# Cosine-similarity attention: five PSUM banks of scores, exponentials of 1536 and 1024 columns in turn, norm words moved into the second output bank, and the norms of 26 pairs summed on VectorE

## The chip, the core and the metric

The kernel runs on one core of one Trainium2 chip. The metric is the device time of one execution in microseconds (us). A core has five engines with instruction streams of their own: TensorE (PE in the profile, its weight loads PEld), VectorE (DVE), ScalarE (ACT), GpSimd (POOL) and SyncE (SP), which here only issues transfers. They meet through semaphores. TensorE writes its results to PSUM, which has 8 banks of 512 float columns on 128 partitions; the other engines read them there.

## The reference

For 8 batches of 12 heads, with 512 rows of 64 numbers each, the rows of Q and K are normalised, their products are divided by tau = 0.1 and go through a softmax, and V is averaged with the weights:

```python
batch, heads, seq, dim = 8, 12, 512, 64
Q_norm = Q / (np.linalg.norm(Q, axis=-1, keepdims=True) + 1e-10)
K_norm = K / (np.linalg.norm(K, axis=-1, keepdims=True) + 1e-10)
scores = np.einsum('bhqd,bhkd->bhqk', Q_norm, K_norm) / tau
weights = np.exp(scores - np.max(scores, axis=-1, keepdims=True))
weights = weights / (np.sum(weights, axis=-1, keepdims=True) + 1e-10)
out = np.einsum('bhqk,bhkd->bhqd', weights, V)
```

The scores are cosines times 10, so the kernel leaves out the maximum: no exponential can overflow.

## The kernel before

Two heads make a pair, and 48 pairs (0 to 47) follow each other as in a pipeline. The names below are those of the order in the code: a number after the name is the pair, then the part.

- LD and LV load Q, K and V of a pair (SyncE; the first K and pair 1 elsewhere). The buffers of Q and K hold 18 pairs.
- SQ squares Q and K (GpSimd, 1024 columns a pair).
- The sums of the squares over 64 columns come in two ways. For most pairs TensorE adds 16 slices with an identity matrix (SSQ, line 246) and VectorE adds the four columns that are left (RED, line 253). For the eight pairs in `DIRECT` VectorE reduces the squares itself in two instructions of 512 columns (line 240), and there is no SSQ.
- NEW, steps 0 to 5, is a reciprocal square root on VectorE, by a first guess from the bits and two rounds of refinement, for a group of one or two pairs (`GROUPS`). Steps 6 and later write the factors of Q and of K. The words lie in PSUM (`nps`, a bank of its own, five groups in turn) and SBUF (`ys`, `rk`).
- SCL multiplies Q (VectorE) and K (GpSimd) by their factors. TR transposes both on TensorE into the bank `xps`, and EVA copies them to SBUF on VectorE as `qt`. Seven pairs (`XT`) have K transposed by a transfer instead.
- SCO are the scores: for each head of the pair and each of four chunks c of 128 keys a matmul of 64 rows by 512 columns, one PSUM bank. The two heads lie on rows 0 to 63 and 64 to 127, so both can be in the array at once.
- EXP are the exponentials on ScalarE. SCO.s.c fills two banks (both heads of chunk c), EXP.s.c turns the 1024 columns into bf16 weights in `et`. There are two such couples of banks, so SCO.s.c waits for the exponential two before. `et` holds three pairs. Pair 0 has exponentials of 512 columns, and the last couple of pair 47 goes in three parts (`ENDS`, line 472).
- VC makes V bf16 and adds a column of ones (GpSimd). PV.s.h.t multiplies the weights with it: four matmuls of 65 columns for head h and 128 rows t, into the output banks `ops`, one per head. The 65th column is the sum of the weights.
- RCP takes its reciprocal, NRM multiplies (both VectorE), ST stores. PV of the next pair waits for NRM, since there is one set of output banks.

The eight banks are thus: four for scores, two for outputs, one for transposes and norm sums, one for norm words.

Nothing is scheduled at run time. `ORDER` spells out the operations of each engine in their order, and `schedule` and `run` (lines 46 and 60) turn the needs of each operation into waits. An operation that waits holds up all that stands behind it on its engine. At the start TensorE runs dummy matmuls (`warm`, `fill`, line 218).

Of the kernel before, what the change touches and what calls it, by code (L numbers as in the profile page):

```python
# [10 lines left out]
class Op:  # L11
# [6 lines left out]
    def __init__(self, key, eng, needs, emit, slot=None, take=None, until=None, hard=()):  # L18
# [3 lines left out]
        self.slot, self.take, self.until = slot, take, until  # L22
        self.sem, self.val, self.inc, self.used = None, 0, 0, False
# [6 lines left out]
class Program:  # L30
# [15 lines left out]
    def schedule(self):  # L46
# [3 lines left out]
        for e, ops in order.items():  # L50
            before = {}
# [74 lines left out]
def bass_cosine_similarity_attention_kernel(  # L126
# [28 lines left out]
    et = [sb(f"et{i}", [128, NT, 2, SEQ], bf16) for i in range(R_ET)]  # L155
# [11 lines left out]
    sc_ps = nc.alloc_psum_tensor("scps", [128, 4, SEQ], f32)  # L167
# [3 lines left out]
    n_ps = nc.alloc_psum_tensor("nps", [128, R_X, 6 * W], f32)  # L171
# [17 lines left out]

    def src(x, s):  # L190
        b, h = divmod(2 * s, NHEAD)
        return x[b, h : h + 2].rearrange("h (p t) d -> p h (t d)", t=NT)
# [7 lines left out]

    def scores_read(s, c):

        if s < 0:
            return None
        return ("EXP", s, c, 1) if s == 0 else ("EXP", s, c, 2) if (s, c) == (NP - 1, NT - 1) else ("EXP", s, c)

# [14 lines left out]
    for k in range(WARM):  # L221
        dummy(("warm", k), sc_ps[:, 3], ["wz", ("warm", k - 1) if k else None])
# [11 lines left out]
    def sums(s, dst, free):  # L234

        sqs = [k for k in (("SQ", s, 0), ("SQ", s, 1)) if k in P.ops]
        if s in DIRECT:
            for w in range(2):
                P.add(("RED", s, w), "dve", [sqs[min(w, len(sqs) - 1)], free],
                      lambda e, w=w: e.tensor_reduce(  # L240
                          out=dst(w), in_=sq[s % R_SQ][:, 8 * w : 8 * w + 8, :], axis=AX.X, op=ALU.add))
# [10 lines left out]
        P.add(("RED", s, 0), "dve", [("SSQ", s), free],  # L252
# [13 lines left out]
    def scaled(s, w, eng, r, needs):  # L266
# [5 lines left out]
                  in0=qk[iq][:, w].rearrange("p h (t d) -> p h t d", t=NT), in1=r, op=ALU.mult))  # L272
# [17 lines left out]
    def head():  # L290

        k_ps = o_ps[:, 0, :].bitcast(bf16).rearrange("p (t x) -> p t x", x=128)
        rq = [o_ps[:, 1, 384:388], sc_ps[:, 1, 0:4]]
        for h in range(2):
            for w, x, eng in ((0, Q, "sp"), (1, K, "act")):
                P.add(("LD", 0, w, h), eng, [], lambda e, w=w, x=x, h=h: e.dma_start(
                    out=qk[0][:, w, h], in_=src(x, 0)[:, h]), slot=f"first{w}{h}")
        for h in range(2):
# [15 lines left out]
            P.add(("SCL", 0, 0, h), "dve", [("EX", 0, 0, h)], lambda e, h=h, q_out=q_out, view=view: e.tensor_tensor(  # L314
# [32 lines left out]
    def norms(g):  # L347
# [20 lines left out]
        for k, step in enumerate(steps):  # L368
# [8 lines left out]
            P.add(("NEW", g, k), "dve", needs, step)  # L377
        for k, (i, j) in enumerate(k_runs(g), 7):
            P.add(("NEW", g, k), "dve",
                  [("NEW", g, 5)] + ([("SCL", p, 1) for p in range(first[g - R_X], first[g - R_X] + sizes[g - R_X])] if g >= R_X else []),  # L380
                  up(k_norms(g, i, j), m + 8 * i, m + 8 * j))

    def pair(s):
        g = group[s]
        iq, iv, iqt, iet, io = (s % r for r in (R_QK, R_V, R_QT, R_ET, R_O))
# [20 lines left out]
        if s == 1:  # L406
            rq = o_ps[:, 1, 384:392]
# [4 lines left out]
            r = xr[1][:, :] if eng == "pool" else o_ps[:, 1, 392:400]  # L412
# [13 lines left out]
        if s:  # L426
            nb = NT if s in XT else 2 * NT
            if s in XT:
                P.add(("XT", s), "sp", [("SCL", s, 1), *[key("SCO", s - R_QT, NT - 1, *y) for y in ((), (0,), (1,))]],
# [4 lines left out]
            P.add(("EVA", s), "dve", [("TR", s), *[key("SCO", s - R_QT, NT - 1, *y) for y in ((), (0,), (1,))]],  # L434
# [4 lines left out]
        last_pair = s == NP - 1  # L439
        for c in range(NT if s == 0 else 0):  # L440
            b = c % 2
            for h in range(2):
                P.add(("SCO", 0, c, h), "pe",
                      [("EVA", 0, 0, h), ("EVA", 0, 1, h), ("EXP", 0, c - 2, h) if c > 1 else None,
                       ("fill", FILL[0] - 1) if c == 1 and h and FILL[0] else None],
                      lambda e, b=b, c=c, h=h: e.matmul(  # L446
                          out=sc_ps[:, 2 * b + h, :], lhsT=qt[0][64 * h : 64 * h + 64, 1, c, :],
                          rhs=qt[0][64 * h : 64 * h + 64, 0, :, :], start=True, stop=True))
        for i, (c, h) in enumerate(START if s == 0 else ()):
# [3 lines left out]
                      out=et[0][:, c, h, :], in_=sc_ps[:, 2 * b + h, :], func=ACT.Exp,  # L453
                      scale=xr[0][:, NT * h + c : NT * h + c + 1]), hard=[("EX", 0, 1, h)])
        for c in range(NT if s else 0):
            b = c % 2

            def sco(e, c=c, b=b):
                for h in range(2):
                    last = e.matmul(  # L460
                        out=sc_ps[:, 2 * b + h, :], lhsT=qt[iqt][64 * h : 64 * h + 64, 1, c, :],
                        rhs=qt[iqt][64 * h : 64 * h + 64, 0, :, :], start=True, stop=True)
                return last

            P.add(("SCO", s, c), "pe",
                  [("SCO", s, c - 1) if c else None, ("EVA", s), key("XT", s),
                   scores_read(s, c - 2) if c >= 2 else scores_read(s - 1, c + 2)], sco)
            before = [("SCO", s, c), scores_read(s, c - 1) if c else scores_read(s - 1, NT - 1), key("PV", s - R_ET, 1, NT - 1)]
            if last_pair and c == NT - 1:
                for i, (h, lo, hi) in enumerate(ENDS):  # L470
                    P.add(("EXP", s, c, i), "act", before + [key("EXP", s, c, i - 1)],
                          lambda e, c=c, b=b, h=h, q=slice(128 * lo, 128 * hi): e.activation(
# [87 lines left out]
WARM = 17  # L560
# [177 lines left out]
```

## Time and profile before

| what | value |
|---|---|
| median of 3 runs | 192.63 us (192.46 to 193.04) |
| the profiled execution | 192.5 us |
| its span, first to last instruction | 190.8 us |
| granted TensorE clock, mean | 0.996 |
| bytes read and written | 37.75 MB, 12.58 MB |
| VectorE instructions, ScalarE instructions | 456, 214 |

The profile's groups read: line, engine, operation, output and input tiles, shape, count; then busy time in us and the mean ns of one; then the idle time of the engine just before them and what ended it. Timeline rows read: start in us, length in us, then the group and its count. Rows of windows give the stretch, its length, the busy time of each engine asked for with the number of instructions, the granted clock, the share of the transfer engines and GB/s. A row of waits reads: who waited, for whom, us in total, how often, the longest.

### The profile page before, as it was taken

The numbers are of one execution on the slowest core, as the hardware profiler recorded it, in microseconds if no ns is written. First come the engines' busy times: TensorE is split into PE (matmuls) and PEld (weight loads), VectorE is DVE, ScalarE is ACT, GpSimd is POOL, SyncE is SP. The second block draws the span as 40 slices with busy tenths as digits, with TensorE's granted clock in tenths as the row PEclk, the third lists the DMA queues.
The fourth block names the chain that finished last, engine by engine and source line by source line (L and its number), as shares of the span: only waits on it lengthen the run. The fifth ranks groups of instructions, "written<-read, shape, count | busy, mean of one in ns | idle before, by whom it ended". The sixth has DMA issues, their size and how long they took to land.

```text
span 190.8 us, 7108 instructions
## 1 busy us (share of the span) xinstructions
PE 178.1 (93%) x2943; PEld 116.5 (61%) x2943; DVE 149.1 (78%) x456; ACT 182.1 (95%) x214; POOL 163.3 (86%) x151
## 2 busy tenths in 40 slices
PE   7899999999998999999989899999999999999982
PEld 5466666656664666666646566566656666656551
DVE  1699987789788899679967988789789598976623
ACT  5699999999999999999999999999999999999991
POOL 6799989999999998999899999999899999970000
PEclk9999999999999999999999999999999999999998
DMA  5999999689999999999989999489375899210167
GB/s 170 300 359 351 351 355 368 177 277 322 375 361 282 311 339 366 239 349 347 365 274 283 353 356 379 134 247 342 105 248 170 248 363 352 66 55 3 55 212 233
DMA packets 55872, 51.71 MB, mean 271 GB/s; under 512 B 6944, under 2 KB 55712, under 8 KB 55840
## 3 DMA queue, kind: packets, MB, share of 16 engines
q1 hardware_dynamic: 55392, 50.48, 82.6%
q0 software_dynamic: 160, 0.52, 0.8%
q8 instruction: 23, 0.38, 0.8%
q10 hardware_dynamic: 288, 0.26, 0.4%
q14 instruction: 9, 0.07, 0.1%
HBM read 37.75 MB, written 12.58 MB: 264 GB/s over the span
## 4 chain that ended last, share of the span: by engine, by line
ACT 72%; PE 15%; POOL 5%; DVE 3%; DMA 2%; issue 1%; POOLq 0%
ACT et L476 72%; PE scps L460 4%; PE ops L492 3%; POOL sq L231 3%; PE xps L246 3%; DMA qk<-in_Q_dram 2%; PE xps L277 2%; POOL qn L270 1%; PE ops L218 1%; DVE qt L435 1%; POOL vb L481 1%; PE scps L446 1%; DVE ob L536 1%; DVE ob L506 0%; DVE nps L355 0%
## 5 line engine op out<-in xcount | busy, mean ns | idle before, releaser
L476 ACT ACTIVATE et<-scps 128x1024 bf16<-128x1024 f32 x187 | 172.0, 1149 | 0.6 <-PE scps L460 0.6
L231 POOL TENSOR_TENSOR sq<-qk 128x1024 bf16<-128x1024 f32 (+1 forms) x49 | 88.8, 1823 | 2.5 <-DMA qk<-in_Q_dram 2.2
L460 PE MATMUL scps<-qt 64*128 64x512 bf16 x376 | 73.3, 386 | 6.4 <-ACT et L476 4.5
L492 PEld LDWEIGHTS ops<-vb,et 128*128 128x128 bf16 x1504 | 53.3, 98 | 25.2 <-issue 18.7
L492 PE MATMUL ops<-vb,et 128*128 128x65 bf16 x1504 | 67.9, 194 | 0.2
L270 POOL TENSOR_TENSOR qn<-qk,rk 128x512 bf16<-128x512 f32 x44 | 45.4, 1043 | 3.2 <-DVE rk L359 2.9
L435 DVE COPY qt<-xps 128x1024 bf16<-128x1024 bf16 (+1 forms) x47 | 30.5, 648 | 6.3 <-PE xps L277 5.7
L506 DVE TENSOR_TENSOR ob<-ops,rd 128x512 f32<-128x512 f32 x47 | 32.4, 690 | 1.1
L460 PEld LDWEIGHTS scps<-qt 64*128 64x128 bf16 x376 | 18.5, 93 | 23.2 <-ACT et L476 9.2
L270 DVE TENSOR_TENSOR qn<-qk,nps 128x512 bf16<-128x512 f32 x48 | 32.1, 680 | 0.2
L481 POOL TENSOR_SCALAR vb<-vf 128x512 bf16<-128x512 f32 x48 | 29.6, 626 | 0.0
L277 PE MATMUL xps<-ident,qn 128*128 128x128 bf16 x348 | 27.5, 220 | 0.0
L246 PE MATMUL xps<-sq,ident 128*128 128x64 bf16 x624 | 25.0, 192 | 0.9 <-POOL sq L231 0.9
L246 PEld LDWEIGHTS xps<-sq,ident 128*128 128x128 bf16 x624 | 20.6, 97 | 8.2 <-issue 4.1
L277 PEld LDWEIGHTS xps<-ident,qn 128*128 128x128 bf16 x348 | 19.7, 98 | 8.3 <-issue 3.6
L504 DVE RECIPROCAL rd<-ops 128x8 f32<-128x8 f32 x47 | 9.7, 206 | 15.0 <-PE ops L492 14.1
L253 DVE TENSOR_REDUCE nps<-xps 128x16 f32<-128x64 f32 x38 | 8.7, 229 | 7.1 <-PE xps L246 6.8
L240 DVE TENSOR_REDUCE nps<-sq 128x8 f32<-128x512 bf16 x16 | 10.7, 680 | 0.0
L355 DVE SCALAR_TENSOR_TENSOR nps<-nps,ys 128x32 f32<-128x32 f32 (+1 forms) x48 | 9.3, 194 | 1.2
L354 DVE TENSOR_TENSOR nps<-nps,ys 128x32 f32<-128x32 f32 (+1 forms) x48 | 9.3, 193 | 0.9
L218 PE MATMUL scps<-warm_in 128*128 128x256 bf16 x23 | 5.1, 382 | 1.1 <-DVE warm_in L216 1.1
L452 ACT ACTIVATE et<-scps,xr 128x512 bf16<-128x512 f32 x8 | 4.8, 688 | 0.1
(54 smaller groups left out, 49.2 us busy)
## 6 DMA issues: line engine op xcount, KB each, us to landing
vf<-in_V_dram SPq DMA_DIRECT2D x48, 256.0 KB, 5.7
out_dram<-ob SPq DMA_DIRECT2D x47, 256.0 KB, 4.8
qk<-in_K_dram SPq DMA_DIRECT2D x46, 256.0 KB, 5.8
qk<-in_Q_dram SPq DMA_DIRECT2D x46, 256.0 KB, 6.0
qk<-in_Q_dram SPq DMA_DIRECT2D x2, 128.0 KB, 2.7
qk<-in_K_dram ACTq DMA_DIRECT2D x2, 128.0 KB, 2.9
qk<-in_Q_dram POOLq DMA_DIRECT2D x1, 256.0 KB, 4.7
qk<-in_K_dram POOLq DMA_DIRECT2D x1, 256.0 KB, 4.3
```

The source lines that it names most:

```text
L231: emit = lambda e: e.tensor_tensor(out=b, in0=a, in1=a, op=ALU.mult)
L240: lambda e, w=w: e.tensor_reduce(out=dst(w), in_=sq[s % R_SQ][:, 8 * w : 8 * w + 8, :], axis=AX.X, op=ALU.add))
L246: last = e.matmul(out=x_ps[:, 0:64], lhsT=ident[:, :], rhs=sq[s % R_SQ][:, :, 4 * k : 4 * k + 4], start=(k == 0), stop=(k == 15))
L270: lambda e: e.tensor_tensor(out=qn[iqn][:, w].rearrange("p t h d -> p h t d"), in0=qk[iq][:, w].rearrange("p h (t d) -> p h t d", t=NT), i ...
L277: last = e.transpose(dst[:, i, :], qn[s % R_QN][:, b // NT, b % NT].rearrange("p h d -> p (h d)"), ident[:, :])
L435: lambda e: e.tensor_copy(out=qt[iqt][:, :].rearrange("p w t x -> p (w t) x")[:, 0:nb], in_=tb[:, 0:nb]))
L460: last = e.matmul(out=sc_ps[:, 2 * b + h, :], lhsT=qt[iqt][64 * h : 64 * h + 64, 1, c, :], rhs=qt[iqt][64 * h : 64 * h + 64, 0, :, :], sta ...
L476: lambda e, c=c, b=b: e.activation(out=et[iet][:, c, :, :], in_=sc_ps[:, 2 * b : 2 * b + 2, :], func=ACT.Exp, scale=inv_tau))
L481: lambda e: e.tensor_scalar(out=vb[:, iq, :, :, 0:DIM].rearrange("p c h d -> p h c d"), in0=vf[iv][:, :, :].rearrange("p h (c d) -> p h c ...
L492: last = e.matmul(out=o_ps[:, h, 65 * t : 65 * t + 65], lhsT=et[iet][:, c, h, 128 * t : 128 * t + 128], rhs=vb[:, iq, c, h, :], start=(c = ...
L504: lambda e: e.reciprocal(out=rd[io][:, :], in_=grid[:, :, :, DIM]))
L506: lambda e: e.tensor_tensor(out=ob[io][:, :], in0=grid[:, :, :, 0:DIM], in1=rd[io][:, :].unsqueeze(3).to_broadcast([128, 2, NT, DIM]), op= ...
```

## The change

The needs of the work stay; the bank plan, the size of the exponentials, the place of the norm words, the way of some norm sums and all five orders are new.

1. *Scores.* Five banks instead of four. The 376 blocks (pair, chunk, head) of pairs 1 to 47, less the last two, are cut into 151 units of three and two blocks in turn, across the borders of chunks and pairs: `stream`. Even units have banks 0 to 2 and odd units 3 and 4. Units 0, 2, 4 and 150 (`TWO`) have two blocks. SCO.k and EXP.k are now those of unit k; the last two blocks are the unit Z, whose exponential goes in the same three parts as before. There are 72 exponentials of 1536 columns and 79 of 1024, with the 187 of 1024 gone.
2. *Weights.* `et` becomes six slots of five blocks. PV finds its block by `place`.
3. *Outputs and norm words.* The eight output tiles lie 65 columns wide in pairs every 149 columns, so that only the last (head 1, t = 3) is in the second output bank, at its first 65 columns. The norm words (four groups in turn) lie behind it in that bank. Since TensorE and VectorE would then use one bank, VectorE operations on the words are marked `shares`, and the last PV step of a pair waits for the last such operation ahead of the pair's RCP (`after`).
4. *Norm sums.* `DIRECT` has 26 pairs instead of 8, so 18 SSQ are gone and 36 reductions of 512 columns come for 18 of 64.
5. *Start.* 12 filler matmuls instead of 18, into a bank that pair 0 leaves free. On ScalarE and VectorE some of the first operations change places; `one` goes ahead of the loads on GpSimd's queue, and the loads of pair 1 and its squares go K first.

```diff
+                if o.shares:
+                    sharer = o.key
+                if o.after is not None and sharer is not None:
+                    self.ops[o.after].needs.append(sharer)
...
-    R_QK, R_V, R_SQ, R_QN, R_QT, R_ET, R_O = 18, 6, 6, 5, 5, 3, 8
+    R_QK, R_V, R_SQ, R_QN, R_QT, R_ET, R_O = 18, 6, 6, 5, 5, 6, 8
-    R_X = 512 // (6 * W)
+    R_X = 4
...
-    et = [sb(f"et{i}", [128, NT, 2, SEQ], bf16) for i in range(R_ET)]
+    et = sb("et", [128, R_ET, 5 * SEQ], bf16)
...
-    sc_ps = nc.alloc_psum_tensor("scps", [128, 4, SEQ], f32)
+    sc_ps = nc.alloc_psum_tensor("scps", [128, 5, SEQ], f32)
...
-    n_ps = nc.alloc_psum_tensor("nps", [128, R_X, 6 * W], f32)
+    n_ps = o_ps[:, 1, 65 : 65 + R_X * 6 * W].rearrange("p (g x) -> p g x", g=R_X)
...
+    def o_tile(h, t):
+        return o_all[:, 149 * t + 65 * h : 149 * t + 65 * h + 65]
...
+    blocks = [(s, c, h) for s in range(1, NP) for c in range(NT) for h in range(2)]
+    blocks, ends = blocks[:-2], blocks[-2:]
+    stream, place = [], {}
+    while sum(map(len, stream)) < len(blocks):
+        at, k = sum(map(len, stream)), len(stream)
+        stream.append(blocks[at : at + (2 if k % 2 or k in TWO else 3)])
...
+    def scores(k):
+        unit, part = stream[k], k % 2
+        bank = sc_ps[:, 3 * part : 3 * part + len(unit), :]
+        def sco(e):
+            for j, (s, c, h) in enumerate(unit):
+                rows = slice(64 * h, 64 * h + 64)
+                last = e.matmul(out=bank[:, j, :], lhsT=qt[s % R_QT][rows, 1, c, :], rhs=qt[s % R_QT][rows, 0, :, :],
+                                start=True, stop=True)
+            return last
...
+        P.add(("EXP", k), "act",
+              [("SCO", k), ("EXP", k - 1) if k else ("EXP", 0, *START[-1]), ("PV", gone, 1, NT - 1) if gone is not None else None],
+              lambda e: e.activation(
+                  out=et[:, (k // 2) % R_ET, lo : lo + SEQ * len(unit)], in_=bank, func=ACT.Exp, scale=inv_tau), width=len(unit))
...
-DIRECT = {36, 41, 11, 46, 16, 21, 26, 31}
+DIRECT = {36,41,11,46,16,21,26,31,8,13,19,24,29,34,38,44,10,18,23,28,33,40,43,14,20,25}
...
-FILL = (6, 12)
+FILL = 12
+TWO = {0,2,4,150}
```

The new order of TensorE around the units that the prediction speaks of:

```
SCO.5 SSQ.5 SCO.6 TR.3 PV.0.0.3 PV.0.1.0 PV.0.1.1 PV.0.1.2 PV.0.1.3 SSQ.6 SCO.7 SCO.8 SSQ.7 PV.1.0.0
```

A stretch of VectorE's new order, with copy, reciprocal and the steps of a square root in between:

```
EVA.21 RCP.17 NEW.11.7 NRM.17 RED.25.1 RED.25.0 SCL.22.0 NEW.12.0 RCP.18 NEW.12.1 NRM.18 SCL.23.0
```

More of the change, by code (lines that the diff above doesn't have):

```diff
@@ L11, with __init__ @@
 class Op:
-    def __init__(self, key, eng, needs, emit, slot=None, take=None, until=None, hard=()):
+    def __init__(self, key, eng, needs, emit, slot=None, take=None, until=None, hard=(), shares=False, after=None, width=0):
         self.key, self.eng, self.emit = key, eng, emit
@@ L251, in sums @@
         P.add(("SSQ", s), "pe", sqs + ["eye", ("warm", WARM - 1) if s == 1 else None], ssq, take="x", until=("RED", s, 0))
-        P.add(("RED", s, 0), "dve", [("SSQ", s), free],
+        P.add(("RED", s, 0), "dve", [("SSQ", s), *free], shares=s > 1, emit=
               lambda e: e.tensor_reduce(
@@ L452, in pair @@
                   lambda e, c=c, b=b, h=h: e.activation(
[L453 removed]
+                      out=et0[:, c, h, :], in_=sc_ps[:, 3 * b + h, :], func=ACT.Exp,
                       scale=xr[0][:, NT * h + c : NT * h + c + 1]), hard=[("EX", 0, 1, h)])
[L455 to L472, printed above, removed]
[L473 to L477 removed]
         P.add(("VC", s), "pool", [("LV", s), key("PV", s - R_QK, 1, NT - 1), "vone"],
@@ new lines, in last_scores, with sco @@
+    def last_scores(s):
+        n = len(stream)
+        t, lo = qt[s % R_QT], 3 * (n % 2)
+        bank = sc_ps[:, lo : lo + 2, :]
+        def sco(e):
+            for h in range(2):
+                last = e.matmul(out=bank[:, h, :], lhsT=t[64 * h : 64 * h + 64, 1, NT - 1, :],
+                                rhs=t[64 * h : 64 * h + 64, 0, :, :], start=True, stop=True)
+            return last
+        P.add(("SCO", "Z"), "pe", [("SCO", n - 1), ("EVA", s), key("XT", s), ("EXP", n - 2)], sco)
+        old = n - 2 * R_ET
+        gone = stream[old][-1][0]
+        for i, (h, lo, hi) in enumerate(ENDS):
+            P.add(("EXP", "Z", i), "act",
+                  [("SCO", "Z"), ("EXP", "Z", i - 1) if i else ("EXP", n - 1), ("PV", gone, 1, NT - 1)],
+                  lambda e, x=SEQ * h + 128 * lo, n_=128 * (hi - lo), h=h, lo=lo: e.activation(
+                      out=et[:, (n // 2) % R_ET, 3 * SEQ * (n % 2) + x : 3 * SEQ * (n % 2) + x + n_],
+                      in_=bank[:, h, 128 * lo : 128 * lo + n_], func=ACT.Exp, scale=inv_tau))
```

376 lines of the change are left out of this document (196 added, 180 removed).

## The prediction

> **What bounds the kernel now.** I read the busy totals first, then the chain of waits, then the exponentials one stretch at a time, because an engine that is 95% busy on average may still be waiting in the stretch that matters.
>
> ```profile
> span 190.8 us, 7108 instructions
> ...
> PE 178.1 (93%) x2943; PEld 116.5 (61%) x2943; DVE 149.1 (78%) x456; ACT 182.1 (95%) x214; POOL 163.3 (86%) x151
> ...
> ACT 72%; PE 15%; POOL 5%; DVE 3%; DMA 2%; issue 1%; POOLq 0%
> ...
> L476 ACT ACTIVATE et<-scps 128x1024 bf16<-128x1024 f32 x187 | 172.0, 1149 | 0.6 <-PE scps L460 0.6
> ```
>
> ScalarE holds 72% of the chain that ended last, all of it the 187 exponentials of 1024 columns; the rest of the chain is the start, before they run unbroken. Records of neighbours overlap (1149 ns long, yet 172.0/187 = 0.920 us each), so a record's length is not its price. The price is the distance between neighbours, read from merged rows of the ScalarE timeline (start, length, count):
>
> ```profile
> 13.15 1.02 ACT L476 ACTIVATE et<-scps 128x1024 bf16<-128x1024 f32 x1
> ...
> 14.97 14.98 ACT L476 ACTIVATE et<-scps 128x1024 bf16<-128x1024 f32 x16
> 30.17 27.75 ACT L476 ACTIVATE et<-scps 128x1024 bf16<-128x1024 f32 x30 [0.21 <-PE scps L460]
> ...
> 58.28 127.52 ACT L476 ACTIVATE et<-scps 128x1024 bf16<-128x1024 f32 x139 [0.37 <-PE scps L460]
> ...
> 179.15 6.66 ACT L476 ACTIVATE et<-scps 128x1024 bf16<-128x1024 f32 x7
> 185.47 1.38 ACT L472 ACTIVATE et<-scps 128x512 bf16<-128x512 f32 x3
> ```
>
> An exponential with an empty engine ahead takes 1.02 us. So the last 139 cost (127.52 - 1.02)/138 = 0.917 us each, and that is the bare price: over 127 us nothing made ScalarE late that this average could hide. The 48 before them took 58.28 - 13.15 = 45.13 us, at 0.917 they need 44.0: **1.1 us of stalls, all before 58 us**. The kernel is thus 13.15 us of start, 187 x 0.917 = 171.5 us of exponentials, 1.1 us of stalls, and 190.8 - 185.8 = 5.0 us of end. Whatever shortens it must shorten the second term, or the small third one.
>
> **The exponentials.** The end gives the price of an instruction as such: the three parts at L472 do 1024 columns (512 + 256 + 256) and end at 186.85, the exponential before them at 185.81. That is 1.04 us, against 0.917 in one instruction, so two extra instructions cost 0.123 us: 0.06 us each, and 0.856 us for 1024 columns. An exponential of 1536 columns should then cost 0.061 + 1.5 x 0.856 = 1.345 us. The change makes 72 of 1536 columns and 79 of 1024 (units 0, 2, 4 and 150 have two blocks, as every odd unit has): 72 x 1.345 + 79 x 0.917 = 169.3 us against 171.5. **Term: -2.2 us**, 36 instructions fewer. Above, 1536 columns could cost a flat 1.5 x 0.917 = 1.375 us, and the term is 0. Below, the instruction cannot be cheaper than its columns, 1.284 us, which gives -6.6. I take -2.2: the rows it rests on are the same form of instruction in the same kernel.
>
> [...]
>
> **TensorE.** The rows that price its pieces (each start to the next start):
>
> ```profile
> 9.11 0.60 PE L446 MATMUL scps<-qt 64*128 64x512 bf16 x3
> 9.65 0.83 PE L218 MATMUL ops<-warm_in 128*128 128x256 bf16 x6
> ...
> 12.72 0.39 PE L460 MATMUL scps<-qt 64*128 64x512 bf16 x2
> 13.04 0.65 PE L246 MATMUL xps<-sq,ident 128*128 128x64 bf16 x16
> 13.62 0.39 PE L460 MATMUL scps<-qt 64*128 64x512 bf16 x2
> ...
> 14.73 0.62 PE L277 MATMUL xps<-ident,qn 128*128 128x128 bf16 x8
> 15.29 0.39 PE L460 MATMUL scps<-qt 64*128 64x512 bf16 x2
> 15.61 0.66 PE L492 MATMUL ops<-vb,et 128*128 128x65 bf16 x16
> 16.20 0.39 PE L460 MATMUL scps<-qt 64*128 64x512 bf16 x2
> ```
>
> Two scores on the two halves of the rows run together: 0.32 us until the next instruction, 0.39 to the result. Three cost 0.54 and 0.60, since the third shares a half with the first. A norm sum (SSQ) takes 0.58, a transpose (TR) 0.56, sixteen PV matmuls 0.59 (a PV step of four 0.15 at most). The score work goes from 188 x 0.32 = 60.2 to 72 x 0.54 + 80 x 0.32 = 64.5 us, +4.3; the 18 further norm sums that leave (26 pairs against 8) take 18 x 0.58 = 10.4 with them. TensorE ends 6 us lighter, which by itself buys nothing where ScalarE does not wait for it. What matters is the place. A three-bank unit is scored while ScalarE works on a two-bank one, in 0.917 us instead of 1.345. Of that 0.60 go to the scores, 1.02 - 0.917 = 0.10 to an exponential that starts on an empty engine, and 13.15 - (12.72 + 0.39) = 0.04 to the hop to ScalarE, as an estimate as much back: 0.13 us are left, where two scores in the same gap leave 0.34. The average cover is good; a single late TensorE step in front of a three-bank unit is paid almost in full.
>
> In the new order one gap is too full by counting alone: between the scores of units 6 and 7 stand TR.3, the last five steps of PV.0 with 20 matmuls, and SSQ.6: 0.54 + 0.56 + 20 x 0.037 + 0.58 = 2.42 us, where 0.037 is 0.59/16. Scores 7 may start when exponential 5 is done and have to be there when 6 ends: 0.917 + 1.345 less 0.39 and 0.18 of hops = 1.69. So 0.7 us late (0 if ScalarE itself is late there for another reason; up to 1.0 if the next gaps, which are nearly full too, add to it). **Term: +0.7 us.** Later on the same count fits everywhere: no stretch of eight or more units asks for more than its exponentials take.
>
> **VectorE and the shared bank.** Its rows, of four stretches, of the operations and of its waits:
>
> ```profile
> 20.00:60.00 40.00, 32.95 (x103) 1.00 1.01 315
> 60.00:100.00 40.00, 33.79 (x106) 1.00 1.02 326
> 100.00:140.00 40.00, 33.40 (x101) 1.00 0.82 269
> 140.00:180.00 40.00, 30.83 (x93) 1.00 0.57 181
> ...
> L240 DVE TENSOR_REDUCE nps<-sq 128x8 f32<-128x512 bf16 x16 | 10.7, 680 | 0.0
> L253 DVE TENSOR_REDUCE nps<-xps 128x16 f32<-128x64 f32 x38 | 8.7, 229 | 7.1 <-PE xps L246 6.8
> L270 DVE TENSOR_TENSOR qn<-qk,nps 128x512 bf16<-128x512 f32 x48 | 32.1, 680 | 0.2
> ...
> DVE rd L504 <- PE ops L492: 14.1, 23, 2.4
> ```
>
> A pair whose squares are summed on VectorE costs two reductions of 10.7/16 = 0.67 us instead of one of 8.7/38 = 0.23. For 18 more pairs that is 18 x (1.34 - 0.23) = +20.0 us, so 149.1 goes to 169.1 of some 189. In the 160 us of the four stretches VectorE was busy 131.0; with +20 it is 151 of about 158, or 95%. Less than that is possible: the new order puts long operations between the short dependent ones of the square roots, and a short one (0.19 us) overlaps a long neighbour. Of its 29 us of idle time there, much was waiting for finished PV sums (14.1 us over the whole span, last row), which is being early, and being early costs nothing. So I put the term at 0, with the rival below for the other side.
>
> The norm words now lie in the bank into which the last PV step of each pair writes. That step waits for the last VectorE operation on these words ahead of the pair's reciprocal. In 33 of 47 pairs the copy of a transpose (0.69 us, another bank) stands between the two on VectorE, so the four matmuls (0.12 us) run beside it. Without that cover VectorE idles 0.12 plus two hops of 0.04, 0.2 us: 14 x 0.2 = 2.8 us of VectorE time, inside the idle time that is left. Behind the waiting step on TensorE stand the next scores, whose slack is the 0.13 us above; here the two edits meet.
>
> **Start and end.** Twelve filler matmuls instead of 18, and on ScalarE one exponential of norms (0.12 us) moved ahead of the wait for the second pair's norms: -0.1 us. The wait itself ends with loads and two squares on GpSimd, which go in the other half's order; I put that at 0, with 0.3 either way. The end has the same three parts and stores: 0. The loads have the same bytes and are issued in another order on SyncE's queue, with 18 buffers of lead: 0. GpSimd keeps its 163.3 us of work:
>
> ```profile
> 100.00:120.00 20.00, 19.38 (x336) 12.87 (x334) 16.73 (x51) 20.00 (x23) 20.00 (x18) 1.00 1.04 343
> ...
> 160.00:180.00 20.00, 18.59 (x308) 11.84 (x306) 15.02 (x43) 20.00 (x23) 10.30 (x12) 1.00 0.25 79
> ```
>
> After the length of the stretch come PE, PEld, DVE, ACT and POOL, and the last shows GpSimd full in mid-span and done 9.7 us before 180, some 17 us ahead of ScalarE. It has to serve pairs 1.3% faster, 2 us over the span, out of those 17: 0. The other stalls I leave at their 1.1 us (0 to 3: two of the early ones wait for norm sums on TensorE that partly move to VectorE, and VectorE is fuller).
>
> **Sum.** -2.2 + 0.7 - 0.1 = -1.6 us. The profiled execution took 192.5 us with its span of 190.8, so 190.9 us, with a span of 189.2. The median of the runs shown is 192.63, so this is 0.9% faster.
>
> **The rivals.**
> *VectorE becomes the bound.* Against it: 33 covered pairs, and before its idle time was mostly being early. For it: if half of the 29 us of idle time stays with 151 us of work, the stretch lasts 165.5 us, 7.5 over its 158; with 6 us saved by overlap it is 1.5 over. In the middle 4.5: 195.4 us. It decides once VectorE's idle time per pair passes (158 - 151)/44 = 0.16 us, about a quarter of the present 29/44 = 0.66.
> [...]
>
> *Three-bank units come late.* TensorE misses the 0.13 us by 0.05 us on average over 72 units: 3.6 us, 194.5. For it: with two banks TensorE waited for ScalarE in only 21 of 188 cases, so it normally arrives after the bank is free. Against it: the two-bank units in between have 0.43 us more than now, in which it can catch up.
>
> ```profile
> PEld scps L460 <- ACT et L476: 9.2, 21, 0.8
> ```
>
> *The longer exponential saves nothing* (1.375 us): 193.1 us with the rest unchanged.
>
> *The early stalls go.* No wait at unit 7 and the 1.1 us gone as well: 189.1 us, in the likeliest case's lower part.
>
> **How the numbers follow.** Likeliest, 0.57: ScalarE still sets the time, 190.9, by itself 189.0 to 192.0. VectorE bound 0.18; late three-bank units 0.15; no saving 0.10. A difference of 0.3%, 0.58 us, is about what a measurement of this kernel can tell from no change. The likeliest case is nearly all faster than that (0.56), and 0.03 of the mild ends of the rivals too: 0.59. Within it: most of no saving and mild cases of the two slow rivals, 0.15. Slower: 0.26. The range reaches from the case without early stalls to the middle of the VectorE case: 189.0 to 195.4.
>
> **What would show it.** Right: a ScalarE timeline with over a hundred microseconds in one piece, at 2.26 us for a unit of 1536 and one of 1024 together; a drawn-out stretch around unit 7 only; 52 reductions of squares at 0.67 us, with VectorE 163 to 169 us busy. Wrong: exponentials of 1536 further apart than 1.36 us; ScalarE idle before three-bank units, released by scores, spread over the span; scores or PV waiting for VectorE with the reciprocal close behind the norm words. GpSimd waiting for norms in the middle of the span would upset what I left at 0.

## The result, and the profile after

| what | before | after |
|---|---|---|
| median of 20 runs | 192.62 us (191.88 to 193.28) | 192.02 us (191.85 to 195.80) |
| ratio after / before | | 0.9969, 95% interval 0.9959 to 0.998 |
| the profiled execution, its span | 192.5 us, 190.8 us | 195.73 us, 193.9 us |

The changed kernel is 0.6 us faster; 1.6 were forecast. Three of its 20 executions took 195.7 to 195.8 us and are left out of the ratio; the profiled one is among them, so its start is some 3.7 us longer than usual.

The head of the page, the chain's shares and the group of the exponentials, after:

```profile
span 193.9 us, 6486 instructions
...
PE 175.4 (90%) x2649; PEld 106.1 (55%) x2649; DVE 160.2 (83%) x474; ACT 180.6 (93%) x178; POOL 163.3 (84%) x151
...
ACT 80%; PE 13%; DVE 4%; issue 1%
...
L544 ACT ACTIVATE et<-scps 128x1024 bf16<-128x1024 f32 (+1 forms) x151 | 169.9, 1285 | 2.4 <-PE scps L530 2.3
```

ScalarE still holds the chain. Its exponentials were 172.0 us of busy time and are now 169.9, 36 instructions fewer. VectorE went from 149.1 to 160.2 us, not to 169. The ScalarE timeline of after (start, length, group and count) shows where the rest of the time is:

```profile
14.37 1.84 ACT L484 ACTIVATE et<-scps,xr 128x512 bf16<-128x512 f32 x3 [1.10 <-PE scps L478]
17.59 7.16 ACT L544 ACTIVATE et<-scps 128x1024 bf16<-128x1024 f32 x7 [1.38 <-PE scps L530]
25.68 162.91 ACT L544 ACTIVATE et<-scps 128x1024 bf16<-128x1024 f32 x144 [0.94 <-PE scps L530]
188.48 1.16 ACT L565 ACTIVATE et<-scps 128x512 bf16<-128x512 f32 x3
```

From unit 7 on, 144 exponentials run in one piece of 162.91 us, 71 of them of 1536 columns and 73 of 1024. At the forecast's 1.345 and 0.917 that is 95.5 + 66.9 = 162.4 us, and the first of a piece costs 0.1 more, so 0.4 us of stalls are left in it. The one large stall is the 0.94 us in front of unit 7, just where it was forecast. But the first unit starts at 17.59 us instead of 13.15, and after the last exponential ends (188.48 + 1.16 = 189.64) the span lasts another 4.27 us, against 3.91 (186.85 to 190.76) before.

So the steady part went as predicted, and what is missing lies at the start and at the end. No execution of the usual length was profiled for this kernel. Its usual span is 190.2 us; less the 172.05 us from the first unit to the end of the last exponential and 4.3 to 4.6 us of end, this leaves 13.6 to 13.9 us for the start, an estimate. TensorE's timeline of after shows why the start was so late in the profiled run:

```profile
5.25 0.64 PE L361 MATMUL ops<-ident,qn 128*64 128x128 bf16 x4
...
9.07 1.06 PE L280 MATMUL xps<-sq,ident 128*128 128x64 bf16 x16
...
15.51 1.49 PE L251 MATMUL scps<-warm_in 128*128 128x256 bf16 x6
16.93 0.61 PE L530 MATMUL scps<-qt 64*128 64x512 bf16 x2
17.47 0.78 PE L280 MATMUL xps<-sq,ident 128*128 128x64 bf16 x16
...
19.72 0.39 PE L530 MATMUL scps<-qt 64*128 64x512 bf16 x2
21.02 0.65 PE L280 MATMUL xps<-sq,ident 128*128 128x64 bf16 x16
```

The same sixteen matmuls of a norm sum last 1.06 us at 9.07 and 0.65 at 21.02, the same two scores 0.61 and 0.39. TensorE worked at half its rate until between 17 and 18 us. In the profile of before it was at full rate from about 4.9 us on (the norm sum at 13.04 took 0.65 us, the six dummies at 9.65 took 0.83, here 1.49). The first transposes, the fillers between them and the first norm sum there:

```profile
4.85 0.44 PE L327 MATMUL ops<-ident,qn 128*64 128x128 bf16 x4
...
5.57 0.50 PE L218 MATMUL scps<-warm_in 128*128 128x256 bf16 x3
...
8.21 0.64 PE L246 MATMUL xps<-sq,ident 128*128 128x64 bf16 x16 [0.44 <-POOL sq L231]
```

### The profile page after: what moved, and what is told of

Its sections match the earlier page's. It is cut to its first block, busy times and chain, and to the rows that moved or that the text cites. A ratio compares the mean times of both kernels' runs of the same rounds, so it can differ in the third digit from the quotient of the medians.

```text
span 193.9 us, 6486 instructions
## 1 busy us (share of the span) xinstructions
PE 175.4 (90%) x2649; PEld 106.1 (55%) x2649; DVE 160.2 (83%) x474; ACT 180.6 (93%) x178; POOL 163.3 (84%) x151
## 4 chain that ended last, share of the span: by engine, by line
ACT 80%; PE 13%; DVE 4%; issue 1%
ACT et L544 80%; PE scps L251 3%; PE xps L280 3%; PE scps L478 2%; PE scps L530 2%; PE ops L500 2%; PE xps L311 1%; DVE ob L515 1%; DVE qt L469 1%; DVE ob L591 0%; DVE qn L304 0%; PE ops L358 0%; DVE rd L513 0%; PE ops L361 0%; PE xps L358 0%
## 5 line engine op out<-in xcount | busy, mean ns | idle before, releaser
L544 ACT ACTIVATE et<-scps 128x1024 bf16<-128x1024 f32 (+1 forms) x151 | 169.9, 1285 | 2.4 <-PE scps L530 2.3
L274 DVE TENSOR_REDUCE ops<-sq 128x8 f32<-128x512 bf16 x52 | 34.6, 680 | 0.0
L304 DVE TENSOR_TENSOR qn<-qk,ops 128x512 bf16<-128x512 f32 x50 | 33.7, 677 | 0.6 <-ACT ops L297 0.6
L515 DVE TENSOR_TENSOR ob<-ops,rd 128x512 f32<-128x512 f32 x47 | 32.3, 688 | 0.7 <-DVE rd L513 0.2
L530 PEld LDWEIGHTS scps<-qt 64*128 64x128 bf16 x374 | 15.8, 93 | 26.1 <-ACT et L544 13.4
L280 PEld LDWEIGHTS xps<-sq,ident 128*128 128x128 bf16 x336 | 12.3, 101 | 6.0 <-issue 4.2
L280 PE MATMUL xps<-sq,ident 128*128 128x64 bf16 x336 | 14.4, 198 | 0.4 <-DVE rd L513 0.3
L389 DVE SCALAR_TENSOR_TENSOR ops<-ops,ys 128x32 f32<-128x32 f32 (+1 forms) x48 | 9.2, 191 | 0.7
L388 DVE TENSOR_TENSOR ops<-ops,ys 128x32 f32<-128x32 f32 (+1 forms) x48 | 9.1, 190 | 0.8
L251 PE MATMUL scps<-warm_in 128*128 128x256 bf16 x29 | 7.3, 417 | 1.7 <-DVE warm_in L249 1.7
L287 DVE TENSOR_REDUCE ops<-xps 128x16 f32<-128x64 f32 x20 | 4.5, 225 | 2.6 <-PE xps L280 2.4
```

The lines of the kernel that those rows point to most:

```text
L251: P.add(key, "pe", needs, lambda e: e.matmul(out=bank[:, 0:256], lhsT=warm_in[:, 0:128], rhs=warm_in[:, :], start=True, stop=True))
L274: lambda e, w=w: e.tensor_reduce(out=dst(w), in_=sq[s % R_SQ][:, 8 * w : 8 * w + 8, :], axis=AX.X, op=ALU.add), shares=s > 1)
L280: last = e.matmul(out=x_ps[:, 0:64], lhsT=ident[:, :], rhs=sq[s % R_SQ][:, :, 4 * k : 4 * k + 4], start=(k == 0), stop=(k == 15))
L304: lambda e: e.tensor_tensor(out=qn[iqn][:, w].rearrange("p t h d -> p h t d"), in0=qk[iq][:, w].rearrange("p h (t d) -> p h t d", t=NT), i ...
L515: lambda e: e.tensor_tensor(out=ob[io][:, :], in0=grid[:, :, :, 0:DIM], in1=rd[io][:, :].unsqueeze(3).to_broadcast([128, 2, NT, DIM]), op= ...
L530: last = e.matmul(out=bank[:, j, :], lhsT=qt[s % R_QT][rows, 1, c, :], rhs=qt[s % R_QT][rows, 0, :, :], start=True, stop=True)
```

## The experiments

All first units, stalls and ends below are read from ScalarE's records. A unit's stall is the distance from the end of the exponential before it to its own end, less 1.343 or 0.917 us.

**Is the profile of after typical?**

The changed kernel as it is. 

> The changed kernel once more, for a profile of an execution whose matmuls reach full rate at the start. Theory: exponentials are 0.917 and 1.343 us apart as in the first profile, the stalls after unit 10 stay under 0.5 us, and the span is near 190.2 us; so some 0.9 us against the forecast 189.2 must lie before unit 10 or behind the last exponential. Rival: they are spread over the units (VectorE or the three-bank scores late), over 0.8 us after unit 10.

Measured: 195.94 us, span 194.2, first unit again at 17.59. This execution is a long one too, so a usual one was not caught. The stalls agree with the first profile to 0.02 us: unit 6 0.10, 7 1.04, 10 0.21, 36 0.08, 56 0.12, 130 0.06. The 0.3 us by which the two spans differ come behind the last exponential, which ends at 189.66 us here and at 189.64 there.

**One dummy more in one row.** `warm.16` goes ahead of the first transpose.

```diff
-        warm.15 TR.0.1.0 TR.0.0.0 TR.0.1.1 SCO.0.0.0 TR.0.0.1 SCO.0.1.0 warm.16 fill.0 SSQ.1
+        warm.15 warm.16 TR.0.1.0 TR.0.0.0 TR.0.1.1 SCO.0.0.0 TR.0.0.1 SCO.0.1.0 fill.0 SSQ.1
```

> One dummy matmul (the seventeenth) moved back ahead of the first transpose, where the kernel before had it. Theory: the executions near 195.7 us come from a TensorE that is still at half rate when the first transposes begin (16 dummies of 0.22 us end too soon); with 17 dummies in a row none is above 193.5 us, and the others stay at 192.0 within 0.3. Rival: those executions have another cause, and about one in six stays near 195.7 us.

Measured: 192.22 us median of 12 (191.52 to 196.81), ratio 0.9984 (0.9956 to 1.0013). The profiled run is of the usual kind: span 190.6, full rate from 7.1 us, first unit at 14.10, the same stalls. But 193.63, 194.88 and 196.81 still occur. One dummy is not the cure; the theory fell.

**The dummies earlier.** In the changed kernel VectorE fills the column of ones (`vone`) before the dummies' input (`wz`), and the first dummy starts at 1.73 instead of 1.11 us.

```diff
-        vone wz RED.0.0.0 SCL.0.0.0
+        wz vone RED.0.0.0 SCL.0.0.0
```

> The changed kernel with two VectorE operations at the start back in the order before: the zeros for the dummy matmuls (wz) ahead of the ones for V (vone). Theory: vone ahead cost 0.6 us of the dummies' start (first dummy at 1.73 us against 1.11), so TensorE came to full rate at 7.2 us instead of 4.5, the first unit's exponential started at 14.1 instead of 13.2, and in some executions full rate was missed until 17 us (195.7 us in all). With wz first the dummies start at 1.1, the first unit at 13.2 to 13.5, the usual executions come down by 0.5 to 0.9 us to 191.1 to 191.5 and the long ones become rarer. Rival: full rate depends on the number of dummies, not on when they start; then the usual time stays at 192.0 and the share of long executions too.

Measured: 193.97 us median (191.63 to 195.23), ratio 0.9998 (0.9954 to 1.0042); 7 of 12 runs took 193.9 us or more, against 4 of 21 of the changed kernel. The long executions became more frequent and not rarer. The dummies now end at 4.7 us, and in the profiled run, a long one, TensorE pauses between the first transposes (one ends at 5.27, the next starts at 5.39), where in the changed kernel they follow each other. A late start of the dummies is not the cause either.

The same step the other way round, in the kernel before (`vone`, which stood further down, put ahead of `wz`): 

> The kernel before with the opposite edit: vone ahead of wz, all else as it was. Theory: first dummy 0.6 us later, usual executions 0.3 to 0.9 us longer than the kernel before (192.4 on this chip), and some near 196 us only if the 18 fillers do not catch it. Rival: no difference, since the kernel before has more dummies.

Measured: 192.59 us (191.96 to 193.43), ratio 0.9991 (0.9964 to 1.0017), none of 12 long; full rate from 5.8 us, first unit at 13.46. The kernel before bears late dummies. Among the things that it has and the changed one lacks are filler matmuls between the first transposes.

**The fillers put back.** `wz` first, 17 dummies in a row, and 17 fillers, six of them among the transposes and first scores of pair 0.

```diff
-FILL = 12
+FILL = 17
...
-        vone wz RED.0.0.0
+        wz vone RED.0.0.0
...
-        warm.15 TR.0.1.0 TR.0.0.0 TR.0.1.1 SCO.0.0.0 TR.0.0.1 SCO.0.1.0 warm.16 fill.0 SSQ.1 fill.1
+        warm.15 warm.16 TR.0.1.0 TR.0.0.0 fill.0 fill.1 fill.2 TR.0.1.1 SCO.0.0.0 fill.3 TR.0.0.1 SCO.0.1.0 fill.4 fill.5 SSQ.1
```

> The changed kernel with wz first and with dummies back between the first transposes: 17 in a row and 17 fillers, six of them ahead of the first norm sum. Theory: TensorE has no gap in which its rate can fail to rise; no execution above 193.5 us, median 191.2 (190.8 to 191.6). Rival: the dummies delay the transposes by as much as they gain, median 192.0 or more.

Measured: 191.89 us (191.54 to 192.59), ratio 0.9963 (0.9936 to 0.999), none of 12 long. The long executions are gone as expected, but the usual time did not fall to 191.2 us: this ratio cannot be told from the 0.9969 (0.9959 to 0.998) of the changed kernel. To separate its two edits, the same with `vone wz` as in the changed kernel: 

> The changed kernel with vone first on VectorE, as it has it, and with the dummies of the previous best version (17 in a row and 17 fillers, three of them after the second transpose). Theory (the fillers left out among the first transposes let TensorE stay at half rate): no execution at 194 us or more, median 191.8 to 192.1, first unit at 13.7 to 14.2 us. Rival (both the later wz and the fewer fillers are needed for the long executions, and the order of vone matters by itself): as after, with one in seven at 194 to 196, or a median 0.3 us over that of the version with wz first.

Measured: 192.0 us (191.46 to 192.64), ratio 0.9991 (0.9972 to 1.001) on a chip where before took 192.26; none of 12 long. The fillers, with `warm.16` in its old place, are enough for none of these 12 to be long; the usual ones did not become faster by an amount that can be told. Over the kernels with the new start and the usual time near 192 us, those without the fillers (the changed kernel and the versions with `warm.16` or `wz` moved) took 193.9 us or more in 13 of 45 executions; those with them (this one, the one before it and the two variants below with one and with two more edits) in 2 of 46; the kernel before in 4 of 104.

The long executions are of two kinds. In 8 of the 13 the mean granted clock was 0.994 to 1.000, as in the profile of after (0.995). In the other 5, in the 2 and in the 4 it was 0.970 to 0.991, as in a run of the last section (0.988) in which TensorE lost its rate again. So the first kind occurs in 8 of 45 executions without the fillers and in none of 46 with them; the second occurs with them, without them and in the kernel before. TensorE's timeline of this version, to be read beside that of after:

```profile
5.37 0.41 PE L361 MATMUL ops<-ident,qn 128*64 128x128 bf16 x4
...
5.94 0.50 PE L251 MATMUL scps<-warm_in 128*128 128x256 bf16 x3
...
8.74 0.63 PE L280 MATMUL xps<-sq,ident 128*128 128x64 bf16 x16 [0.32 <-DVE qt L321]
...
12.38 0.82 PE L251 MATMUL scps<-warm_in 128*128 128x256 bf16 x6
```

Transposes, norm sums and dummies are at full rate from the first transpose on. The first unit still comes at 13.78 us, not 13.15. The row of the first norm sum says why: that of pair 1 starts at 8.74, released by VectorE's copy of pair 0's last transpose. In the kernel before it started at 8.21, as soon as GpSimd had squared pair 1 (6.12 + 2.04 = 8.16); there the transposes and copies were done by then and hidden. In all seven profiles of the new start that have full rate by 7.2 us the first unit starts 5.0 to 5.1 us behind this norm sum, and in six of them the norm sum starts 0.14 to 0.15 us behind the end of the copy. In the old order the distance is 4.9 us and the norm sum follows the squares, which come when the loads do: at 8.21 us in the profile of before, at 8.51 in that with `vone` moved. So single profiles tell the loss at the start to some tenths only.

**The gap at unit 7.** VectorE, TensorE and ScalarE around it, in the timeline of the version with `wz` first and 17 fillers:

```profile
19.83 0.69 DVE L469 COPY qt<-xps 128x1024 bf16<-128x1024 bf16 x1
...
20.44 0.21 DVE L513 RECIPROCAL rd<-ops 128x8 f32<-128x8 f32 x1
...
20.66 0.63 PE L280 MATMUL xps<-sq,ident 128*128 128x64 bf16 x16 [0.26 <-DVE rd L513]
...
21.23 0.82 PE L530 MATMUL scps<-qt 64*128 64x512 bf16 x5
...
21.66 3.30 ACT L544 ACTIVATE et<-scps 128x1024 bf16<-128x1024 f32 x3 [0.93 <-PE scps L530]
```

TensorE is full up to SSQ.6, and SSQ.6 writes the bank `xps` from which VectorE copies TR.3 until 20.52, so it cannot start before; it starts 0.14 us later. Scores 7 stand behind it. The row names the reciprocal, which was issued behind the copy; the copy is what the bank waits for. In the same version, scores 7 moved ahead of SSQ.6:

```diff
-        PV.0.0.3 PV.0.1.0 PV.0.1.1 PV.0.1.2 PV.0.1.3 SSQ.6 SCO.7 SCO.8 SSQ.7
+        PV.0.0.3 PV.0.1.0 PV.0.1.1 PV.0.1.2 PV.0.1.3 SCO.7 SSQ.6 SCO.8 SSQ.7
```

> e5 (the changed kernel with wz first, 17 dummies in a row and 17 fillers) with one operation moved on TensorE: the norm sum of pair 6 goes behind the scores of unit 7 instead of ahead of them. Theory: unit 7 is 1.04 us late because this norm sum stands ahead of its scores and, besides its own 0.58 us, waits 0.38 us for the copy of pair 3's transpose, which holds the bank both use. Moved, unit 7 is at most 0.2 us late, unit 10 at most 0.3, and the time falls by 0.8 to 1.2 us against e5, to 190.9 (190.6 to 191.3). Rival: what is won at unit 7 is lost before unit 10, since the same work stands ahead of a later unit; then units 7 to 14 together are still 0.9 us late or more, and the time stays at 191.9.

Measured: 191.9 us (191.52 to 194.42), ratio 0.9981 (0.996 to 1.0001). Unit 7 falls from 1.04 to 0.39, and units 8 and 9 come at 0.19 and 0.72: 1.6 us for units 6 to 10 against 1.37 before the move. This move shifts the stall and does not remove it: what was won at unit 7 is lost before unit 10. Whether every order of this work would cost as much was not tried.

**The end.** In the version with scores 7 moved, PV of pairs 43 and 44 and the transpose of pair 47 reordered, so that PV might run less late:

```diff
-        PV.43.0.0 PV.43.0.1 PV.43.0.2 PV.43.0.3 SCO.144 PV.43.1.0 TR.47 PV.43.1.1 PV.43.1.2 PV.43.1.3 SCO.145 SCO.146
-        PV.44.0.0 PV.44.0.1 PV.44.0.2 PV.44.0.3 PV.44.1.0
+        PV.43.0.0 PV.43.0.1 PV.43.0.2 PV.43.0.3 PV.43.1.0 SCO.144 PV.43.1.1 PV.43.1.2 PV.43.1.3 TR.47 SCO.145 PV.44.0.0 PV.44.0.1
+        SCO.146 PV.44.0.2 PV.44.0.3 PV.44.1.0
```

> e6 with six PV steps of pairs 43 and 44 moved ahead of scores and of the last transpose near the end. Theory: the end is longer than before (4.3 us from the last exponential's end against 3.9) because pair 46's outputs are divided only after the last exponential is done; these steps bring that forward by 0.1 to 0.4 us, and the time falls by as much against e6, with no new stall above 0.15 us at units 144 to 150. Rival: every later PV still starts behind the same scores, and the division of pair 46 stays within 0.1 us of where it was; no change against e6.

Measured: 191.99 us (191.84 to 194.59), ratio 0.9999 (0.9969 to 1.0028); no gain over the 191.9 us without the move. Its profile caught a long start of the second kind (last section).

Next, in the version with `wz` first and 17 fillers, the last block of pair 46, which comes in a unit of three with two blocks of pair 47, was made the end of a unit: `TWO = {0, 2, 148, 150}`. 

> As the version with wz first and 17 fillers, but with TWO = 0, 2, 148, 150, so that unit 4 has three blocks, all units up to 147 end one block further on, and the last exponential of pair 46 is unit 147 and not 148 with two blocks of pair 47. The count of exponentials is unchanged. Theory A (the end is longer because the last block of pair 46 comes in a unit of three with pair 47, so PV.46 starts 0.9 us later against the last exponential): PV.46 starts 0.3 us or more earlier against the end of the last exponential than 2.3 us, and the stretch from there to the end of the span falls from 4.3 to about 4.0 us. Theory B (PV.46 waits for the normalisation of pair 45 just as long, because the one set of output banks lags): PV.46 stays where it is, 4.2 to 4.4 us. Either way stalls may move by 0.3 us, since the place of scores in the order is not replanned.

Measured: 194.94 us (194.76 to 195.08), ratio 1.0141 (1.011 to 1.0172). The end did not move (PV.46 starts 2.3 us ahead of the last exponential's end in both, and 4.3 us follow it): theory B. The 3 us are stalls, 5.1 us instead of the 2.2 in the profile of the version that it is made from, spread over the middle (unit 16 1.04, 94 0.54, 124 0.42, 142 0.70): shifting the units by one block against an order that was not replanned makes TensorE late.

Then both obstacles were taken away: that version without PV, reciprocal, normalisation and store of pair 45, whose outputs are thus left out, and with PV.46.0 ahead of the scores of unit 150. 

> As the kernel with two blocks in unit 148, but PV, reciprocal, normalisation and store of pair 45 are left out, and PV.46.0 goes ahead of the scores of unit 150: neither the late block nor the lag of the output banks holds PV.46. Theory (these two are what the end has lost): PV.46 done and normalised before the last exponential ends, VectorE free for pair 47, and 3.8 to 4.0 us from the end of the last exponential to the end of the span, as in the kernel before (3.9). Rival (the three last exponentials, PV.47 and the last store set the end by themselves in the new bank plan): 4.2 to 4.4 us still.

Measured: 194.44 us in its one run. PV.46 starts 3.42 us ahead of the last exponential's end instead of 2.33, yet 4.42 us follow it, as the rival says. The chain of waits of that run (start, length, what):

```profile
187.19 0.29 PE scps L579 x4
187.48 0.12 PE xps L579 x4
...
187.91 0.26 PE xps L579 x8
188.17 0.03 issue
188.19 0.24 DVE rd L591 x2
188.43 0.40 DVE ob L593
...
189.20 0.29 DVE ob L593
```

The 32 matmuls of pair 47 all follow the exponential of unit 150, which ended at 187.14, and VectorE's six operations follow them. In the kernel before, six of the 32 ran among those of pair 46. The two ends, from their chains of waits, first the kernel before, then the version with 17 fillers alone:

```profile
186.46 0.20 PE nps L521 x4
186.66 0.02 issue
186.69 0.20 DVE rd L534
...
187.76 0.29 DVE ob L536
```

```profile
185.04 0.22 DVE rd L513
185.26 0.02 issue
185.28 0.65 DVE ob L515
185.94 0.05 issue
185.98 0.14 DVE rd L589
...
186.88 0.29 DVE ob L591
```

VectorE ends 188.05 - 186.85 = 1.20 us behind the last exponential before, and 187.17 - 185.75 = 1.42 here, since the normalisation of pair 46 (L515) stands ahead of those of pair 47. It is 1.20 or 1.21 in all three profiles with the old banks and 1.42 to 1.44 in all ten with the new ones and pair 45. Without pair 45 it is 189.49 - 188.18 = 1.31. So some 0.1 of the 0.2 us is the lag of PV.46, and the other 0.1, by the order of the rows, that of PV.47. The rest of the longer end comes behind the last normalisation, where the store took 2.7 us before and 2.8 to 3.1 here. In the run with four banks and 26 pairs below, which has the old end, it took 3.2, so no difference of the store is shown. With a store of 2.7 us, and not 3.1, the run without pair 45 would have come to 4.0 us, so by itself it does not decide between theory and rival.

**The parts of the change alone.** Five banks with the eight pairs in `DIRECT` as before, so that 18 norm sums are back on TensorE: 

> e5 with only the 8 pairs of the kernel before reduced on VectorE; the norm sums of the other 18 are on TensorE again, placed ahead of a score unit near their old reductions. Theory: the gain is the fewer exponentials alone and moving norm sums only makes room on TensorE; VectorE busy falls by 16 to 20 us, and the time is longer than e5 by 0.5 to 4 us through late three-bank units (the stalls after unit 14 rise from 0.3 us to over 0.8). Rival: TensorE had the room anyway; the time is e5's within 0.3%.

Measured: 203.75 us, ratio 1.0589 (1.0551 to 1.0627). That is far more than the 0.5 to 4 us expected. TensorE 179.8 us busy, VectorE 144.3. ScalarE lost 13.8 us in stalls of 0.1 to 1.2 us from unit 6 to 124. Its waits (who, for whom, us, times, longest):

```profile
ACT et L544 <- PE scps L530: 9.7, 20, 1.1
```

And four banks with 26 pairs in `DIRECT`, with the 18 norm sums out of TensorE's order: 

> The kernel before with the norms of the 26 pairs reduced on VectorE and their norm sums taken off TensorE, nothing else. Theory: VectorE has the room (busy 149 to some 167 us) and ScalarE sets the time, so it is that of the kernel before within 0.3%, at most 0.5% longer. Rival: VectorE becomes the bound in the middle; ScalarE shows stalls of over 2 us between 60 and 180 us, where the kernel before has none, and the time is over 1% longer.

Measured: 200.67 us, ratio 1.0449 (1.0405 to 1.0494). VectorE 165.3 us busy; stalls of 7.9 us, the largest 1.56 at exponential 84. Some 1.5 us of them, at exponentials 58 and 59, fall into the 3.4 us from 68.5 us on in which the granted clock was 0.50 (last section); the mean clock of all four runs is 0.982 to 0.991, which points to such stretches in each, and they are part of this price.

```profile
ACT et L476 <- PE scps L460: 5.4, 8, 1.5
```

Each half alone costs 8 to 11 us. Five banks need a lighter TensorE, and the norm sums on VectorE need an order made for them. In both runs the orders were not replanned, so they bound what the halves are worth in the given order, not at their best.

## Why the prediction was right or wrong

*The exponentials, -2.2 us: right.* The 1536 columns cost 1.343 us from end to end (forecast 1.345) and 1024 cost 0.917. That is 0.065 us an instruction, where the forecast had 0.06. The flat 1.375 would have given no gain.

*Unit 7, +0.7: right in place and cause, mis-sized.* Units 6, 7 and 10 stall by 0.11 + 1.04 + 0.21 = 1.37 us. The count of instructions gave 0.7; it left out that SSQ.6 waits for the copy of TR.3 out of the bank that both use, and that the next gaps catch nothing up. The forecast had allowed up to 1.0.

*Other stalls, left at 1.1: mis-sized the other way.* Beyond unit 10 they are 0.27 us. So 1.7 us of stalls in all against 1.8 forecast: two errors that cancel, which is luck. The 1.1 us were those of one execution, besides: the kernel before with `vone` moved has 0.4 us of stalls.

*VectorE, 0: right.* It rose by 11 us and not by 20. The lengths of its records added up rose as counted, from 168.1 to 187.3 us, but 27.0 us of them overlap instead of 19.0. In the four stretches from 20 to 180 us it was busy 144.5 us where I expected 151. The rival of 195.4 us does not occur in the order given; with 26 pairs and an order not made for it (200.67 us) something like it does, without VectorE being full on average (143.7 us of 160).

*Three-bank units late: did not happen.* TensorE waited for ScalarE more often than before, 39 times for its weight loads, so it is early:

```profile
PEld scps L530 <- ACT et L544: 13.4, 39, 0.9
```

*Start, -0.1: the step that failed.* "Twelve filler matmuls instead of 18" was costed at nothing beyond the matmuls themselves, and the wait at the end of the start at 0, with 0.3 either way, since it was to end with loads and squares. The new order has that wait end with the transposes and copies of pair 0, and without the fillers TensorE can stay at half rate (until 17.8 us in the profile of after). Against 13.15 us in the profile of before, the first unit starts 0.95 us later in the usual profile without fillers (14.10, with one dummy moved) and 4.4 in the long one. With the fillers back 0.5 to 0.6 are left, the norm sum behind the copy.

*End, 0: failed, by less.* "The end has the same three parts and stores" left out VectorE. It ends 0.2 us later against the last exponential, since PV.46 and PV.47 come later. The whole end is 0.36 to 0.67 us longer than in the profile of before; what exceeds the 0.2 is not shown to be more than chance.

The sum, from the version with 17 fillers alone against the profile of before: first unit +0.63, from there to the end of the last exponential 171.97 against 173.70 us, -1.73, end +0.36: together -0.74, and the spans are 190.02 and 190.76. The forecast for the middle was -2.2 + 0.7 = -1.5. Against the profile of the kernel before with `vone` moved (13.46, 173.04 and 3.97 us) it is +0.32 - 1.08 + 0.30 = -0.46. The start and the end thus cost 0.6 to 1.0 us together, and where the smaller figure holds, the kernel before had fewer stalls to begin with. This account rests on profiles: no run got the missing 1 us back.

## What to carry to other kernels

A price per instruction and a count of each gap predicted the 172 us of exponentials to 0.2 us, with the help of two errors that cancel; the 18 us around them, costed by "same parts, so 0", held most of the error. Where a change touches dummy matmuls or the first transposes, ask which rate TensorE has when the first real work arrives (here the same norm sum took 1.06 or 0.65 us), and what has to be finished before the first long wait ends. A change in several parts that were planned together can be worse in each part alone: here each half cost over 8 us in the order at hand.

## What the runs showed of the hardware

TensorE's rate at the start has to be read from like instructions. Windows of TensorE in the profile of after (stretch, length, busy time, granted clock, share of the transfer engines, GB/s):

```profile
5.00:10.00 5.00, 4.83 (x39) 1.00 0.97 324
10.00:17.00 7.00, 7.00 (x46) 1.00 1.09 353
```

The clock reads 1.00 where the same matmuls last 1.06 us instead of 0.65. The trace's record of the granted clock starts only where the full rate does: at 17.8 us in this profile, 13.7 with `wz` first alone, 7.1 with `warm.16` moved, 7.0 and 5.2 in the two versions with fillers, and 4.9 in the kernel before, 5.8 with its `vone` moved. Where full rate came by 7.2 us its moment did not set the first unit, which kept its 4.9 to 5.1 us behind the norm sum of pair 1. At 13.7 and 17.8 it took 7.0 and 8.5 us behind it (first units at 16.01 and 17.59).

The rate can also be lost again, and then the granted clock shows it (0.50 in the window below). In the profile of the kernel with PV.43 reordered, a load came late, and TensorE paused for the squares of pair 1 (timeline, then a window):

```profile
7.57 0.39 PE L251 MATMUL scps<-warm_in 128*128 128x256 bf16 x2
9.55 0.65 PE L280 MATMUL xps<-sq,ident 128*128 128x64 bf16 x16 [1.58 <-POOL sq L264]
...
10.56 0.60 PE L251 MATMUL scps<-warm_in 128*128 128x256 bf16 x2
11.09 1.04 PE L478 MATMUL scps<-qt 64*128 64x512 bf16 x3
...
14.24 0.62 PE L311 MATMUL xps<-ident,qn 128*128 128x128 bf16 x8
```

```profile
10.62:14.02 3.40, 3.40 (x26) 0.50 1.10 365
```

After 1.58 us of pause two dummies take 0.60 us and no longer 0.39; the full rate was back at 14.0 us (eight transposes in 0.62 us, against 1.04 in the profile of after), and the first unit came at 16.08. With four banks and 26 pairs the same happened from 68.5 to 71.9 us. In the 3.4 us ahead of these two stretches TensorE was busy for 1.8 and 1.9 us.

Both of these half-rate stretches lasted 3.4 us. At the start of the kernel before, the 17 dummies come 0.21 us apart from 1.11 to 4.50 (0.11 for the six at 9.65), and the transposes behind them 0.06 us apart. In the profile of after 16 dummies come 0.21 us apart from 1.73 to 4.90, but the transposes behind them still 0.11 us apart. What sets the moment of full rate is not shown. In the second row of this section TensorE was busy for all 7.00 us and stayed at half rate, so busy time as the profile counts it does not decide, and pauses between the matmuls do not explain the long start. And stretches in which TensorE was busy for over half of the time (1.8 and 1.9 of 3.4 us) were followed by half rate. What the fillers, dummies on all 128 rows, do between scores on 64 rows and transposes was not tried apart, so why they help stays open.
